# Another sequence for three groups of matmuls: stick-breaking's values, the shared keys and values, banded attention's queries

## The chip, the cores and the metric

The kernel runs on one core of one Trainium2 chip. The metric is the device time of one execution in microseconds (us); the lower the better. TensorE does the matmuls (PE in the profile, its weight loads PEld), VectorE (DVE) and ScalarE (ACT) the elementwise work, GpSimd (POOL) a few small operations and the accumulating loads, and SyncE (SP) issues the plain loads.

## What is computed

A decoder trunk of two layers on 256 rows of 1024 float32 values. Each layer is a half-step SwiGLU FFN, an attention, and another half-step FFN; layer 0 has stick-breaking attention, layer 1 sliding-window attention over keys and values that are computed once, from the stream after layer 0. Cut from the reference:

```python
for layer in range(DEPTH):                     # DEPTH = 2
    h = h + 0.5 * swiglu(rms_norm(h, ffn1_norm[layer]), ffn1_w_in[layer], ffn1_w_out[layer])
    hn = rms_norm(h, mix_norm[layer])
    if layer < N_A_LAYERS:
        qkv = (hn @ sb_w_qkv[layer]).reshape(B, S, 3, SB_HEADS, HEAD_DIM)
        o = stick_breaking_attention(qkv[:, :, 0], qkv[:, :, 1], qkv[:, :, 2])
        h = h + o.reshape(B, S, SB_HEADS * HEAD_DIM) @ sb_w_o[layer]
    else:
        q = rotary((hn @ swa_w_q[j]).reshape(B, S, SWA_Q_HEADS, HEAD_DIM), pos)
        o = sliding_window_sink_attention(q, k_shared, v_shared, swa_sinks[j])
        h = h + o.reshape(B, S, SWA_Q_HEADS * HEAD_DIM) @ swa_w_o[j]
    h = h + 0.5 * swiglu(rms_norm(h, ffn2_norm[layer]), ffn2_w_in[layer], ffn2_w_out[layer])
    if layer == N_A_LAYERS - 1:
        kv = (rms_norm(h, kv_norm) @ kv_w).reshape(B, S, 2, SWA_KV_HEADS, HEAD_DIM)
        k_shared, v_shared = rotary(kv[:, :, 0], pos), kv[:, :, 1]
return rms_norm(h, final_norm)
```

The model has 16 heads of 64, 4 shared key/value heads, a window of 128 and 2816 hidden columns in each FFN.

## The kernel before

**Tiles and precision.** The 256 rows are two tiles (t = 0, 1) of 128. Every dense product runs as three matmuls on split operands: a megabyte of weights lands in a `raw` buffer, ScalarE casts it to `w_hi` in two halves (L335), VectorE subtracts to give `w_lo` (L337), and TensorE adds x_hi w_hi + x_lo w_hi + x_hi w_lo in a PSUM bank (`step`, L354; all matmuls are issued at L224). There are five raw buffers and ten slots of the pool WP for split weights, that is five weights of a hi and a lo.

**Stages.** Four FFNs with the two attentions between them: FFN, stick-breaking, FFN, FFN, banded attention, FFN. At the end of a stage `finish(t)` adds the residual into `hN` (L453), takes the root of the mean square, scales (`xs`, L440), transposes in TensorE (L386) and splits into `xT_h` (L392) and `xT_l` (L393); the next stage's products of tile t need these. An FFN's block 0 is plain (gate and up, tile by tile), block 1 is narrow (256 columns), blocks 2 to 5 are Strassen-like (`strassen`, L607): four weights are loaded, sums of weights are made in the raw buffers, two by VectorE (L618) and two by accumulating loads from GpSimd's queue (`fetch`, L622). `sums` makes their sums of x from the transposes. `out(n)` multiplies a block's result by `w_out`.

**Stick-breaking** (L761). `values(j)` makes one half of the value columns for both tiles; four groups of heads follow, each with a projection of queries and keys (32 steps of three 256-column matmuls) and two `heads` chains of tasks (scores, ScalarE's functions, cumulative sums, values). `values(0)` stands ahead of group 0, `values(1)` ahead of group 2.

**Shared keys and values** (`shared_kv`, L883). `operands` normalizes `hN` with another gain into `xkv_h`, `xkv_l` through the bank `tr`; 48 matmuls in two banks, a rotation (`rotary`, L873) and transposes through `tr` give `kT_s` and `v_s`. It runs inside the third FFN, behind block 0.

**Banded attention** (L917). `queries(c)` makes 256 query columns (four heads) for both tiles in the banks `qb[0]` and `qb[1]`: 24 matmuls for each tile, a rotation on VectorE (L878 to L881), two transposes back into the same bank (L953), a copy to `qT`. `heads(g, i)` handles two heads of group g: scores for both tiles in the banks `zp[n % 2]`, maxima, exponentials, normalization, transposes (L1022 to L1024) and the product with `v_s`. `out_proj` follows an order written out by hand.

**What sets the order.** Nothing is issued as it is written. Each `T(engine, duration, fn, r=, w=, prio=, lat=)` adds a task to `Plan`; dependencies follow from what tasks read and write, in the order in which they are added. `plan.order()` then simulates the engines with these durations and latencies; whenever an engine is free it takes the ready task of the least `prio`, by default `plan.pos`, which advances with the dense work (`dense`). The order found is the order in each engine's queue, and on the chip each queue is strictly in order. Loads have a prio of 30,000 ns (`LOADS`) ahead of their place, splits 7,000 ns (`LEAD`).

## Time and profile before

| | us |
|---|---|
| median of three runs (all: 940.67, 942.66, 942.68) | 942.66 |
| time of the profiled execution | 940.34 |
| its span, first to last instruction | 938.6 |
| TensorE busy in it | 923.9 (98%) |
| VectorE busy | 776.4 (83%) |
| ScalarE busy | 597.3 (64%) |
| GpSimd busy | 51.6 (6%) |

The load queues moved 206.06 MB, 220 GB/s in the mean, and the mean granted clock of TensorE was 0.995. The stages, by the timeline: first FFN to 189 us, stick-breaking to 309, second FFN to 485, third to 677, banded attention to 756, fourth FFN to the end. The ends of matmuls are modelled, so holes in TensorE are read from the starts of its instructions rather than from its busy share. A time beside a wait is idle time of the engine that waits, and the releaser named is the one that came last.

### The profile page before, as it was taken

To read this page: it belongs to the slowest core of one execution; us is meant where nothing else is said; L and a number is where in the kernel's file an instruction comes from. 1 tells how busy PE (TensorE), PEld (TensorE's weight loads), DVE (VectorE), ACT (ScalarE), POOL (GpSimd) and SP (SyncE) were. 2 spreads that over 40 slices of the span, in tenths; PEclk is the share of its full clock that TensorE was granted. 3 is DMA by queue.
4 is the path that set the end of the run, shared out by engine and by line. 5 is a ranking of instruction groups with operands and counts; after the bars stand their busy time and mean duration, and the time that the engine had idled before them with its cause. 6 is when DMAs were issued, how large, how long until landed. Compare 5 with 4: busy or idle time off the path is not lost.

```text
span 938.6 us, 12152 instructions
## 1 busy us (share of the span) xinstructions
PE 923.9 (98%) x4660; PEld 764.2 (81%) x4660; DVE 776.4 (83%) x918; ACT 597.3 (64%) x837; POOL 51.6 (6%) x62
## 2 busy tenths in 40 slices
PE   9999999999999999999999999999999999999997
PEld 7888888788898888888887888888878788888885
DVE  7889998656566887999878789998688598799983
ACT  6567676647567656776566567677756475676662
POOL 1011010000000000110000001010000000011000
PEclk9999999999999999999999999999999999999999
DMA  9988999773434676999965498999642257799961
GB/s 319 365 193 253 270 297 267 244 247 98 171 96 131 204 222 183 248 293 294 313 230 188 137 264 206 304 281 281 231 157 91 90 180 201 202 227 310 274 175 45
DMA packets 100205, 206.06 MB, mean 220 GB/s; under 512 B 3762, under 2 KB 24498, under 8 KB 100147
## 3 DMA queue, kind: packets, MB, share of 16 engines
q1 hardware_dynamic: 83104, 171.46, 52.5%
q0 software_dynamic: 16896, 33.56, 21.0%
q8 instruction: 36, 0.59, 0.2%
q10 hardware_dynamic: 146, 0.27, 0.1%
q14 instruction: 23, 0.18, 0.1%
HBM read 204.22 MB, written 1.05 MB: 219 GB/s over the span
## 4 chain that ended last, share of the span: by engine, by line
PE 57%; DVE 16%; issue 2%; DMA 2%; ACT 1%; POOL 0%; POOLq 0%; DVEq 0%; ACTq 0%
PE ps L224 54%; DVE w_lo L337 10%; DVE raw L618 3%; DMA raw<-in_ffn_w_in_dram 1%; PE ps L522 1%; DMA raw<-in_swa_w_q_dram 1%; PE ps L386 1%; DVE aT_l L393 1%; ACT w_hi L335 1%; DVE u L638 0%; DVE m L641 0%; DVE hN L453 0%; DVE p L638 0%; PE ps L953 0%; DVE xs L440 0%
## 5 line engine op out<-in xcount | busy, mean ns | idle before, releaser
L337 DVE TENSOR_TENSOR w_lo<-raw,w_hi 128x1024 fp32r<-128x1024 f32 x412 | 485.8, 1221 | 57.3 <-ACT w_hi L335 57.1
L335 ACT CAST w_hi<-raw 128x1024 fp32r<-128x1024 f32 x412 | 411.8, 1050 | 123.2 <-PE ps L224 71.5
L224 PE MATMUL ps<-w_hi,xT_h 128*128 128x512 f32 (+1 forms) x480 | 184.3, 384 | 0.1
L224 PE MATMUL ps<-w_hi,xT_l 128*128 128x512 f32 (+1 forms) x480 | 181.0, 377 | 1.0 <-DVE xT_l L393 1.0
L224 PE MATMUL ps<-w_lo,xT_h 128*128 128x512 f32 (+1 forms) x480 | 181.1, 377 | 0.0
L224 PE MATMUL ps<-w_hi,aT_h 128*128 128x512 f32 x352 | 138.8, 394 | 0.0
L224 PE MATMUL ps<-w_lo,aT_h 128*128 128x512 f32 x352 | 137.4, 390 | 0.0
L224 PE MATMUL ps<-w_hi,aT_l 128*128 128x512 f32 x352 | 137.2, 390 | 0.0
L224 PEld LDWEIGHTS ps<-w_hi,xT_l 128*128 128x128 f32 x480 | 91.0, 190 | 16.8 <-DVE xT_l L393 1.4
L224 PEld LDWEIGHTS ps<-w_hi,xT_h 128*128 128x128 f32 x480 | 91.1, 190 | 16.3 <-issue 0.9
L224 PEld LDWEIGHTS ps<-w_lo,xT_h 128*128 128x128 f32 x480 | 90.9, 189 | 16.5
L224 PE MATMUL ps<-w_hi,S_h 128*128 128x512 f32 x256 | 101.6, 397 | 0.0
L224 PE MATMUL ps<-w_lo,S_h 128*128 128x512 f32 x256 | 100.0, 391 | 0.0
L224 PE MATMUL ps<-w_hi,S_l 128*128 128x512 f32 x256 | 99.8, 390 | 0.0
L618 DVE TENSOR_TENSOR raw<-raw 128x1024 f32<-128x1024 f32 x64 | 77.7, 1223 | 1.1
L224 PEld LDWEIGHTS ps<-w_lo,aT_h 128*128 128x128 f32 x352 | 66.1, 188 | 13.9
L224 PEld LDWEIGHTS ps<-w_hi,aT_l 128*128 128x128 f32 x352 | 66.2, 188 | 13.3
L224 PEld LDWEIGHTS ps<-w_hi,aT_h 128*128 128x128 f32 x352 | 66.2, 188 | 13.1
L623 POOL DMA_DIRECT2D raw<-in_ffn_w_in_dram x32 | 41.0, 1282 | 526.8 <-ACT w_hi L335 171.6
L224 PEld LDWEIGHTS ps<-w_lo,S_h 128*128 128x128 f32 x256 | 48.1, 188 | 10.1
L224 PEld LDWEIGHTS ps<-w_hi,S_l 128*128 128x128 f32 x256 | 48.2, 188 | 9.3
L224 PEld LDWEIGHTS ps<-w_hi,S_h 128*128 128x128 f32 x256 | 48.1, 188 | 9.2
(155 smaller groups left out, 1007.8 us busy)
## 6 DMA issues: line engine op xcount, KB each, us to landing
raw<-in_ffn_w_in_dram SPq DMA_DIRECT2D x76, 1024.0 KB, 7.5
raw<-in_ffn_w_out_dram SPq DMA_DIRECT2D x44, 1024.0 KB, 5.0
raw<-in_ffn_w_in_dram POOLq DMA_DIRECT2D x32, 1024.0 KB, 9.2
raw<-in_sb_w_qkv_dram SPq DMA_DIRECT2D x12, 1024.0 KB, 5.3
raw<-in_ffn_w_in_dram SPq DMA_DIRECT2D x16, 512.0 KB, 5.1
raw<-in_ffn_w_in_dram SPq DMA_DIRECT2D x16, 256.0 KB, 5.6
raw<-in_sb_w_o_dram SPq DMA_DIRECT2D x4, 1024.0 KB, 4.9
raw<-in_swa_w_q_dram SPq DMA_DIRECT2D x4, 1024.0 KB, 8.7
```

The lines of the kernel that those rows point to most:

```text
L224: PE.matmul(ps, lhsT=lhsT, rhs=rhs, start=start, stop=stop, skip_group_check=True)
L335: T("ACT", act(m), lambda sl=sl: ACT.copy(out=flat(hi)[:, sl], in_=flat(raw)[:, sl]), r=[(raw, i) for i in rs] + first, w=[(hi, i) for i i ...
L337: T("DVE", dve(m), lambda sl=sl: DVE.tensor_sub(out=flat(lo)[:, sl], in0=flat(raw)[:, sl], in1=flat(hi)[:, sl].bitcast(F32)), r=[(raw, i) ...
L386: PE.transpose(out=bank.ap[:, i * P:(i + 1) * P], in_=s, identity=ident)
L393: T("DVE", dve(n), lambda: DVE.tensor_sub(out=lo[2](), in0=src(), in1=hi[2]().bitcast(F32)), r=B(bank) + [hi[0:2]], w=[lo[0:2]])
L522: PE.transpose(out=tr.ap[:, i * P:(i + 1) * P], in_=m.ap[:, i * P:(i + 1) * P], identity=ident)
L618: T("DVE", dve(m), lambda sl=sl: DVE.tensor_add(out=flat(dst)[:, sl], in0=flat(dst)[:, sl], in1=flat(src)[:, sl]), r=[(src, k) for k in ks ...
L623: T("POOL", 1500, lambda: nc.gpsimd.dma_start(out=dst.ap, in_=src, accum_op=ALU.add), w=[(dst, 0), (dst, 1)], prio=plan.pos - LOADS, lat=F ...
```

## The change

In stick-breaking all four value products come first, both halves for tile 0 and then both for tile 1. In the third FFN the shared keys and values are added behind block 1 and `out(0)` rather than behind block 0, with the position of their operands set back by 8,000 ns. In banded attention queries are made for one group and one tile at a time, in a sequence written out by hand; queries(1, 0) uses a bank of `zp` for its product and `qb[0]` for its transposes. The hand-written order of the output projection takes six of the eight k ahead instead of four. In the planner a plain load is costed at 330 instead of 250 bytes per ns, and an accumulating load no longer at a latency of 10,000 ns but at 500 ns and a stretch of SP's line at 170 bytes per ns, for which no instruction is issued.

```diff
--- before.py
+++ after.py
@@ -36,7 +36,8 @@
 PAIRS = 5
 RAWS = 5
 PIECES = 2
-FETCH = 10000.0
+ADDING = 170.0
+PLAIN = 330.0
 BY_DMA = False
 DMA3 = True
 FSUMS = 5000.0
@@ -295,7 +296,7 @@
 
 
     def dma(src, dst, nbytes, w, prio, name=None):
-        T("SP", nbytes / (300.0 if prio < -8e5 else 250.0), lambda: nc.sync.dma_start(out=dst(), in_=src), w=w, prio=prio)
+        T("SP", nbytes / (300.0 if prio < -8e5 else PLAIN), lambda: nc.sync.dma_start(out=dst(), in_=src), w=w, prio=prio)
 
     def gain(vec):
         g = G4.get([P, D], F32, "gain")
@@ -621,7 +622,8 @@
 
             def fetch(dst, src):
                 T("POOL", 1500, lambda: nc.gpsimd.dma_start(out=dst.ap, in_=src, accum_op=ALU.add), w=[(dst, 0), (dst, 1)],
-                  prio=plan.pos - LOADS, lat=FETCH)
+                  prio=plan.pos - LOADS, lat=500.0)
+                T("SP", P * 2048 * 4 / ADDING, lambda: None, w=[(dst, 0), (dst, 1)], prio=plan.pos - LOADS)
 
             def product(bank, raw, xs, first, last, at=0.0):
                 w = split(raw)
@@ -716,10 +718,10 @@
             if n == 0:
                 if "s" in blocks:
                     sums()
-                if kv:
-                    kv(ring, tr)
             elif n < last and kind != "s":
                 out(n - 1)
+            if kv and n == 1:
+                kv(ring, tr)
         S8.put(SH, SL)
 
 
@@ -772,15 +774,17 @@
             ring.append(ring.pop(0))
             return ring[-1]
 
-        def values(j):
-            ws = [weight([(slice(0, 512), wv[:, 4 * i:4 * i + 4, 2 * D + 512 * j:2 * D + 512 * j + 512])], 4, 512) for i in range(2)]
-            for t in range(NT):
-                b = bank_()
-                for i in range(2):
-                    four(b, ws[i], lambda kk: of_x(t, 4 * i + kk), i == 0, i == 1)
-                    if t == 1:
-                        WP.put(*ws[i])
-                copy_act(lambda t=t: v.ap[:, t, half(j)], lambda b=b: b.ap, 512, B(b), [(v, (t, j))])
+        vw = {}
+
+        def values(j, t):
+            b = bank_()
+            for i in range(2):
+                if (j, i) not in vw:
+                    vw[j, i] = weight([(slice(0, 512), wv[:, 4 * i:4 * i + 4, 2 * D + 512 * j:2 * D + 512 * j + 512])], 4, 512)
+                four(b, vw[j, i], lambda kk: of_x(t, 4 * i + kk), i == 0, i == 1)
+                if t == 1:
+                    WP.put(*vw[j, i])
+            copy_act(lambda: v.ap[:, t, half(j)], lambda: b.ap, 512, B(b), [(v, (t, j))])
 
         def heads(g, i):
             n = 2 * g + i
@@ -835,10 +839,10 @@
                 sl_ = slice(2 * g, 2 * g + 2)
                 part_to(ob, (oh, g, lambda: oh.ap[:, sl_]), (ol, g, lambda: ol.ap[:, sl_]), 512, lambda: two(ob.ap))
 
-        values(0)
+        for t in range(NT):
+            for j in range(2):
+                values(j, t)
         for g in range(4):
-            if g == 2:
-                values(1)
             ws = [weight([(slice(0, 256), wv[:, :, s * D + 256 * g:s * D + 256 * g + 256])], KD, 256) for s in range(2)]
             for b in range(2):
                 ps = bank_()
@@ -888,7 +892,10 @@
                 normed(t, rstds[t], gk, [tr, tr], kh, kl)
 
         def run(ring, tr):
+            at_ = plan.pos
+            plan.pos -= 8000.0
             operands(tr)
+            plan.pos = at_
             wv = by_k(kv_w)
             bs = [ring[0], ring[1]]
             ring[:] = [ring[2], ring[0], ring[1]]
@@ -929,31 +936,39 @@
         NM, SM, ES = [tiny(2 * H) for _ in range(3)]
         T("ACT", 1300, lambda: ACT.preload_act_table_set("natural_log_exp_and_others"), w=[(consts, "tbl")])
 
-        def queries(c):
-            w = weight([(slice(0, 256), wv[:, :, 256 * c:256 * c + 256])], KD, 256)
-            for t in (1, 0) if c else (0, 1):
-                b = qb[t]
-                for k in range(KD):
-                    (sh, sl), keys = of_x(t, k)
-
-                    def run(k=k, sh=sh, sl=sl, b=b):
-                        r_h, r_l = w[0].ap[:, k], w[1].ap[:, k]
-                        mm(b.ap[:, 0:256], sh(), r_h, k == 0, False)
-                        mm(b.ap[:, 0:256], sl(), r_h, False, False)
-                        mm(b.ap[:, 0:256], sh(), r_l, False, k == KD - 1)
-                    dense(360, run, r=[(w[0], k // 4), (w[1], k // 4)] + keys, w=B(b))
-                if t == (0 if c else 1):
-                    WP.put(*w)
-                qr, tmp = STG.get([P, 4, HD], F32, "qr"), STG.get([P, 4, HD], F32, "qr_t")
-                rotary(lambda qr=qr: qr.ap, tmp, lambda b=b: b.ap[:, 0:256].rearrange("p (n d) -> p n d", n=4), t, 2, 4, B(b), B(qr))
-                STG.put(tmp)
-
-                def run(b=b, qr=qr):
-                    for i in range(2):
-                        PE.transpose(out=b.ap[:, i * P:(i + 1) * P], in_=qr.ap[:, 2 * i:2 * i + 2].rearrange("p a d -> p (a d)"), identity=ident)
-                T("PE", 218, run, r=B(qr) + ID, w=B(b))
-                STG.put(qr)
-                copy_act(lambda t=t: qT.ap[:, 2 * c:2 * c + 2, ts(t)], lambda b=b: b.ap[:, 0:256].rearrange("p (a b) -> p a b", a=2), 256, B(b), [(qT, (c, t))])
+        qw = {}
+
+        def queries(c, t):
+            if c in qw:
+                w = qw.pop(c)
+                last = True
+            else:
+                w = qw[c] = weight([(slice(0, 256), wv[:, :, 256 * c:256 * c + 256])], KD, 256)
+                last = False
+
+
+            b, bt = zp[1][0] if (c, t) == (1, 0) else qb[t], qb[t]
+            for k in range(KD):
+                (sh, sl), keys = of_x(t, k)
+
+                def run(k=k, sh=sh, sl=sl):
+                    r_h, r_l = w[0].ap[:, k], w[1].ap[:, k]
+                    mm(b.ap[:, 0:256], sh(), r_h, k == 0, False)
+                    mm(b.ap[:, 0:256], sl(), r_h, False, False)
+                    mm(b.ap[:, 0:256], sh(), r_l, False, k == KD - 1)
+                dense(360, run, r=[(w[0], k // 4), (w[1], k // 4)] + keys, w=B(b))
+            if last:
+                WP.put(*w)
+            qr, tmp = STG.get([P, 4, HD], F32, "qr"), STG.get([P, 4, HD], F32, "qr_t")
+            rotary(lambda: qr.ap, tmp, lambda: b.ap[:, 0:256].rearrange("p (n d) -> p n d", n=4), t, 2, 4, B(b), B(qr))
+            STG.put(tmp)
+
+            def run():
+                for i in range(2):
+                    PE.transpose(out=bt.ap[:, i * P:(i + 1) * P], in_=qr.ap[:, 2 * i:2 * i + 2].rearrange("p a d -> p (a d)"), identity=ident)
+            T("PE", 218, run, r=B(qr) + ID, w=B(bt))
+            STG.put(qr)
+            copy_act(lambda: qT.ap[:, 2 * c:2 * c + 2, ts(t)], lambda: bt.ap[:, 0:256].rearrange("p (a b) -> p a b", a=2), 256, B(bt), [(qT, (c, t))])
 
         def view(buf, t0, t1, h0, h1):
             return buf.ap.rearrange("p (t h) -> p t h", t=2)[:, t0:t1, h0:h1]
@@ -1042,14 +1057,15 @@
                 sl_ = slice(2 * g, 2 * g + 2)
                 part_to(o, (oh, g, lambda: oh.ap[:, sl_]), (ol, g, lambda: ol.ap[:, sl_]), 512, lambda: two(o.ap))
 
-        for g in range(4):
-            queries(g)
-            for i in range(2):
-                heads(g, i)
+
+        for what, a_, b_ in (("q", 0, 0), ("q", 0, 1), ("h", 0, 0), ("q", 2, 0), ("q", 1, 0), ("h", 0, 1),
+                            ("q", 1, 1), ("h", 1, 0), ("h", 1, 1), ("q", 2, 1), ("h", 2, 0), ("h", 2, 1),
+                            ("q", 3, 1), ("q", 3, 0), ("h", 3, 0), ("h", 3, 1)):
+            (queries if what == "q" else heads)(a_, b_)
         T("ACT", 1300, lambda: ACT.preload_act_table_set("silu_and_others"), w=[(consts, "tbl")])
         WP.put(qT)
         out_proj(w_o, oh, ol, [qb, ob], finish,
-                 [(0, range(4), (0, 1)), (1, range(4), (1,)), (0, range(4, 8), (0, 1)), (1, range(4, 8), (1,)), (1, range(8), (0,))],
+                 [(0, range(6), (0, 1)), (1, range(6), (1,)), (0, range(6, 8), (0, 1)), (1, range(6, 8), (1,)), (1, range(8), (0,))],
                  lambda t, k: [(oh, k // 2), (ol, k // 2)])
         S8.put(oh, ol)
 
```

## Rows read from the trace of the kernel before

**Rows 1.** The page, part 1: busy us (share of the span) and instructions.

```profile
PE 923.9 (98%) x4660; PEld 764.2 (81%) x4660; DVE 776.4 (83%) x918; ACT 597.3 (64%) x837; POOL 51.6 (6%) x62
```

**Rows 2.** The chain that ended last: start us, us, what.

```profile
303.31 11.58 PE ps L224 x51
```

**Rows 3.** Timeline, TensorE, 256-column projections: start us, us, engine line op.

```profile
202.15 0.28 PE L224 MATMUL ps<-xT_h,w_hi 128*128 128x256 f32 x1
...
213.55 0.28 PE L224 MATMUL ps<-xT_h,w_lo 128*128 128x256 f32 x1
```

**Rows 4.** TensorE's waits: us in total, times, longest us.

```profile
PE ps L522 <- DVE m L513: 1.7, 1, 1.7
```

**Rows 5.** Timeline, TensorE, entry of stick-breaking, tile 1's values.

```profile
195.37 0.39 PE L224 MATMUL ps<-w_hi,xT_h 128*128 128x512 f32 x1
196.77 0.50 PE L224 MATMUL ps<-w_hi,xT_l 128*128 128x512 f32 x1 [1.01 <-DVE xT_l L393]
```

**Rows 6.** Timeline, TensorE, third FFN, first block.

```profile
507.66 0.39 PE L224 MATMUL ps<-w_lo,xT_h 128*128 128x512 f32 x1
509.78 0.66 PE L522 MATMUL ps<-ident,m 128*128 128x128 f32 x4 [1.73 <-DVE m L513]
```

**Rows 7.** Timeline, TensorE, entry of banded attention.

```profile
679.85 0.28 PE L224 MATMUL ps<-w_lo,xT_h 128*128 128x256 f32 x1
...
681.52 1.32 PE L386 MATMUL ps<-ident,xs 128*128 128x128 f32 x8 [1.40 <-DVE xs L440]
...
683.71 0.56 PE L224 MATMUL ps<-w_hi,xT_h 128*128 128x256 f32 x1
...
686.48 0.28 PE L224 MATMUL ps<-w_hi,xT_h 128*128 128x256 f32 x1
```

**Rows 8.** Windows, entry of banded attention: PE, PEld, DVE, ACT, POOL busy, granted clock, DMA.

```profile
683.70:691.10 7.40, 7.40 (x52) 7.27 (x51) 6.04 (x10) 2.75 (x4) 0.00 (x0) 0.81 0.70 237
```

**Rows 9.** Windows, heads of groups 0 and 1 in stick-breaking.

```profile
213.70:231.90 18.20, 18.20 (x152) 16.63 (x150) 11.23 (x16) 12.10 (x19) 0.00 (x0) 1.00 0.35 116
231.90:249.50 17.60, 17.60 (x102) 13.76 (x102) 10.67 (x15) 12.31 (x19) 0.00 (x0) 1.00 0.36 120
```

**Rows 10.** Timeline, VectorE, third FFN, first block and shared operands.

```profile
500.37 0.75 DVE L440 SCALAR_TENSOR_TENSOR xs<-hN,small,gain 128x512 f32<-128x512 f32 x1
...
503.37 5.76 DVE L337 TENSOR_TENSOR w_lo<-raw,w_hi 128x1024 fp32r<-128x1024 f32 x5
...
516.12 0.69 DVE L393 TENSOR_TENSOR xkv_l<-ps,xkv_h 128x512 fp32r<-128x512 f32 x1 [1.82 <-ACT xkv_h L392]
...
518.63 0.69 DVE L393 TENSOR_TENSOR xkv_l<-ps,xkv_h 128x512 fp32r<-128x512 f32 x1 [1.82 <-ACT xkv_h L392]
```

**Rows 11.** Windows, third FFN up to and through its Strassen blocks.

```profile
512.00:528.00 16.00, 16.00 (x80) 13.26 (x79) 7.77 (x14) 5.51 (x11) 0.00 (x0) 1.00 0.47 161
528.00:546.00 18.00, 18.00 (x87) 14.81 (x86) 17.86 (x24) 11.78 (x17) 1.30 (x1) 1.00 0.71 173
...
546.00:658.00 112.00, 111.90 (x506) 92.43 (x505) 105.14 (x103) 78.52 (x91) 8.92 (x7) 1.00 0.97 274
```

**Rows 12.** Timeline, VectorE, entry of banded attention.

```profile
682.05 0.28 DVE L878 TENSOR_TENSOR qr_t<-ps,rp 128x128 f32<-128x128 f32 x1
...
682.89 0.42 DVE L881 TENSOR_TENSOR qr<-qr,qr_t 128x256 f32<-128x256 f32 x1
...
684.44 2.35 DVE L337 TENSOR_TENSOR w_lo<-raw,w_hi 128x1024 fp32r<-128x1024 f32 x2
```

**Rows 13.** Timeline, VectorE, end of banded attention.

```profile
747.19 1.37 DVE L453 SCALAR_TENSOR_TENSOR hN<-ps,hN 128x512 f32<-128x512 f32 x2 [2.98 <-PE ps L224]
...
754.51 1.28 DVE L393 TENSOR_TENSOR xT_l<-ps,xT_h 128x512 fp32r<-128x512 f32 x2
```

**Rows 14.** The line L623 (accumulating loads), its last row.

```profile
DMA to landing us min/median/max: 8.4/9.2/12.2
```

**Rows 15.** DMA issues: out<-in engine op xcount, KB each, median us to landing.

```profile
raw<-in_ffn_w_in_dram SPq DMA_DIRECT2D x76, 1024.0 KB, 7.5
```

## The prediction

> **What bounds the kernel now.** I read the page first: TensorE counts as busy for 923.9 of 938.6 us [rows 1]. That share says little, since a record lasts longer than the step to the next start: 51 matmuls of 512 columns take 11.58 us, 227 ns each [rows 2], while one record shows 0.39 us; the 256-column ones start every 0.12 us (95 steps from 202.15 to 213.55) [rows 3]. So I looked for starts that come later than this pace. The four FFNs (L459) run on pace nearly throughout; the end is set by the sum of TensorE's work, and only a hole in TensorE can be won. In the list of TensorE's waits no group comes to more than 1.7 us [rows 4]; the timeline gives the holes their true size:
>
> (a) Entering stick-breaking, the second matmul of tile 1's values waits for that tile's `xT_l`: 195.37 to 196.77, 1.40 us instead of 0.23 [rows 5]. Lost: 1.2 us.
>
> (b) In the third FFN's first block the transposes of `m` start 2.12 us after the last matmul instead of 0.23 [rows 6]. Lost: 1.9 us. This wait of the `m` transposes occurs once in the kernel [rows 4], and only this FFN has the shared keys and values behind its first block.
>
> (c) Entering banded attention: 679.85 to 681.52 before the transposes of tile 1's `xs` (1.55 us lost); from there to 683.71 is 2.19 us for eight transposes and a pair (0.8 + 0.1 us on pace), 1.3 us lost; then 12 matmuls take 2.77 us instead of 1.44, 1.3 us lost [rows 7], because the granted clock averages 0.81 there [rows 8], that is half of 2.4 GHz for a part of it. TensorE had just been nearly idle. Together 4.1 us.
>
> **The change, part by part.**
>
> *Values first, by tile.* The same 96 matmuls, 4 loads and 8 casts in another sequence. At the entry there are now 48 matmuls that need tile 0 alone (10.9 us) instead of 24 (5.4 us). Tile 1 was late by 1.2 us, so 5.4 us more cover takes the hole away: **-1.2 us** (from 0 to -1.4, with the slow start behind the transposes). The two more weights needed early take the places in the cast queues that the first query/key weights have now; those are then needed 10.9 us later. What loses its cover: the heads of group 1 were filled by `values(1)`, 48 matmuls of 0.227 us = 10.9 us, and will be filled by group 2's projections, 96 of 0.12 us = 11.5 us. The trace has both kinds of filling: group 0's heads are filled by projections, group 1's by values, and TensorE is busy through both stretches, VectorE at 11.2 of 18.2 and 10.7 of 17.6 us [rows 9]. So 0 there; bounds -0.2 and +0.5.
>
> *Shared keys and values behind the second block.* Nothing is added; the 48 matmuls, the four xs, transposes and copies, two weights and the rotation all move behind 10.9 us of block 1 and 10.9 us of `out(0)`, with the operands queued 8 us ahead. In VectorE's queue the five weight halves from 503.37 on hold back the product `m`, and VectorE is late at that point because it also does the shared xs at 500.37 (0.7 us) after the sums [rows 10]. Without it and with the same mix as FFNs two and four, which show no such wait, the hole closes: **-1.9 us**. What is hidden anew: the operands go through one bank, one after the other, 2.5 us each (xkv_l at 516.12, 518.63) [rows 10], four of them 10 us; they may start when block 1's second transposes have left `tr`, and `out(0)`'s 48 matmuls are 10.9 us long, so they just fit; if not, the ready Strassen products go first. VectorE is half idle in 512 to 528 (7.8 of 16 us), full in 528 to 546, and 94% busy through the Strassen blocks (105.1 of 112 us) [rows 11]. The moved work is about 12 us on VectorE (four xs and four low halves of 0.6, four weight halves of 1.2, two rotations of 1.3); it leaves the half idle stretch for one 14 to 22 us later that is nearly full, and hands its place to work that was done there. I take 0, since both lie ahead of the same Strassen block and TensorE's work between them is unchanged; bounds 0 and +1.9 (a hole like (b) again, behind the rotation and its transposes). If TensorE needs the keys' transposes before VectorE has rotated, everything behind them in its queue waits, the first Strassen products too.
>
> *Banded attention's queries.* At the entry TensorE now has queries(0,0), (2,0) and (1,0) on tile 0: 72 matmuls, 8.6 us, against 24 (2.9 us). Not all can run in the hole. queries(2,0) uses the same bank as (0,0), which comes free after a rotation of 1.26 us (682.05 to 683.31 [rows 12]), two transposes and a copy: 682.6 at the earliest, 684.5 as now. queries(1,0) has a bank of its own, but its weight is third, and the third weight's low halves come from VectorE at 684.4 to 686.7 now [rows 12]; the queue is likely to take one of them into its wait for the root at 680. By my count 72 query matmuls are done at 688.3 instead of 691.1, with the clock not falling, or less: **-2.8 us**, bounds -4.1 (all of (c)) and -0.5 (nothing but part of the clock's loss). A page speaks against this order: the Trainium skill, Perfetto Trace Analysis, Optimizing Tensor Performance (Matmuls), wants independent groups to rotate through different banks so that emptying one overlaps the next group's matmuls. By that rule alone (2,0) would fill nothing and (c) would shrink by (1,0)'s 2.9 us at most; my -2.8 agrees with it.
>
> At the other end the output projection keeps 30 matmuls behind tile 0's last one instead of 36 (the list now takes six k of tile 1 before tile 0's last two): 30 x 0.227 + 0.8 for the transposes = 7.6 us of cover for a chain that takes 8.2 us (hN at 747.19 to the first half of xT_l at 755.15, and 0.2 before it [rows 13]): **+0.6 us**, bounds 0 and +0.9. When exactly the heads run costs nothing as long as the output projection's matmuls remain to fill between them; the stretch of the heads, 691 to 743, has no such hole now, and if that filling ran out each head's latency would show.
>
> *The planner's costs.* PLAIN, ADDING and the shorter latency emit no instruction; they reorder all queues. For an accumulating load the plan has 1.5 + 10 = 11.5 us now, and 1.5 + 0.5 + 6.2 + 2.0 = 10.2 us after when SP's line is free. They land in 8.4 to 12.2, median 9.2 us [rows 14], so both figures are mostly on the safe side. Plain megabytes go from 4.2 + 2.0 to 3.2 + 2.0 us against a median of 7.5 for the FFN's w_in [rows 15], which is hidden by the five raw buffers that are loaded well ahead. I take 0; bounds below.
>
> **Sum** against the profiled execution (span 938.6, time 940.3): -1.2 - 1.9 - 2.8 + 0.6 = -5.3, so 935.0. The median of the runs shown is 942.7, 2.3 us above the profiled one, so the forecast is **937.3 us**. Changes under 0.3% (2.8 us) can't be told from none.
>
> **Rivals.**
>
> 1. *The bank chain wins in banded attention.* (2,0) and (1,0) come too late, and later (1,1), (2,1) and (3,1) queue for one bank: the part gives 0 instead of -2.2 net. For it: VectorE is 82% busy from 683.7 to 691.1 (6.0 of 7.4 us [rows 8]) and every rotation passes through it. Against: (1,0) has its own bank. Time 939.6.
> 2. *The hole (b) moves.* The rotation and transposes of the shared keys meet a full VectorE and TensorE waits 1.9 us before the first Strassen block. For it: 17.9 of 18 us busy in 528 to 546 [rows 11]. Against: the 8 idle us of VectorE in 512 to 528, which other splits can use in its place. Time 939.2. With rival 1 as well: 941.5, no change.
> 3. *Slower: the new load costs are too hopeful.* ScalarE's queue is in order; a cast (L335) placed before its accumulating load lands holds every cast, silu and staging copy behind it, and VectorE, which works behind ScalarE, has about 7 us to spare per FFN [rows 11]. There are 32 such loads. If each is awaited 1.3 us longer (11.5 - 10.2), that is 41.6 us, less 4 x 7 hidden = +14, so 951 us with the gains. It decides from about 8 us lost, 0.25 us per load above the slack. For it: the last load of each FFN lands late (up to 12.2 us), in front of the next stage's weights. Against: the median of 9.2 is below both costs.
>
> **How the numbers follow.** The forecast, all three gains within their bounds (-3.5 to -7.4, 935.3 to 939.2): 0.58. Rival 1: 0.14, rival 2: 0.10, both: 0.06, rival 3: 0.12. Rivals 1 and 2 alone lie just beyond 2.8 us; I count 0.15 of their 0.24 as faster. So faster 0.73, same 0.09 + 0.06 = 0.15, slower 0.12. The range reaches from a little below the best case, for the runs' own spread of 2 us, to where both rivals hold: 933.5 to 942.5.
>
> **What would show it.** (a) no wait of TensorE for xT_l ahead of the first projections, two groups of 24 value matmuls before tile 1's; (b) m's transposes on pace in the third FFN, and no wait near the shared keys' transposes; (c) 256-column matmuls between 680 and 684, the granted clock at 1.00 and the first scores half a us or a us nearer to the last FFN matmul with more query matmuls ahead of them; at the end a wait of about half a us before the fourth FFN. I am wrong if the Strassen stretches grow (112 us each now), or if the heads' stretch takes more time than the entry gives back.

## The result, and the profile after

The changed kernel takes **935.42 us** (median of 6 runs, 934.89 to 937.01) against 941.30 us for the kernel before, run beside it (6 runs): ratio **0.9938, 95% interval 0.9925 to 0.9951**, so 5.9 us faster. The forecast was 937.3 us in a range of 933.5 to 942.5, made of -5.3 us against the kernel before. The profiled execution took 935.5 us with a span of 933.7 us; that is 4.9 us less than the span of before.

Since only a hole in TensorE can be won, the execution is cut into stages at the first matmul of each, read from TensorE's timeline:

```
us                   start  FFN 1   stick-br.  FFN 2   FFN 3   banded  FFN 4 + end
before               11.27  177.77  119.57     176.12  192.37  78.95   182.52
after                12.98  178.00  118.01     176.01  189.99  76.33   182.40
after - before       +1.71   +0.23   -1.56      -0.11   -2.38  -2.62    -0.12
```

The three edited stages give back 6.6 us. The start (up to the first projection) took between 10.6 and 13.7 us in the profiles of this study without regard to the edit, and the first FFN 177.4 to 178.6 us in those profiles of the kernel before with one part that left it alone; the others agree within 0.8 us where nothing is changed, stick-breaking within 0.1, with one exception: banded attention takes 77.79 us in e10_kvw_later, which doesn't edit it, against 78.9 to 79.3 (the reason stands in the last section). So one profile is good for the stages, to about a us, and the runs for the total. Since spans differ by their start, times of two profiles are compared below from the first matmul of the stage. Of all executions, one of e5_old_costs (2,372 us, against 934.7 to 937.5 in its others) lies apart and is in no figure.

Line numbers are those of each kernel: L225 after is L224 before, L968 is L953. Page, part 1, and TensorE's waits (us in total, times, longest), in reply to [rows 1] and [rows 4]:

```profile
PE 923.0 (99%) x4660; PEld 763.0 (82%) x4660; DVE 776.8 (83%) x918; ACT 596.8 (64%) x837; POOL 51.7 (6%) x62
```

```profile
PE ps L523 <- DVE m L514: 1.1, 1, 1.1
...
PE ps L968 <- DVE qr L885: 0.5, 1, 0.5
...
PE ps L387 <- DVE xs L441: 0.2, 1, 0.2
```

The busy share again says nothing. The 1.7 us wait of `m` is replaced by one of 1.1 us, which has the same name but stands elsewhere (below); the wait for `xT_l` ahead of the first projections is gone.

TensorE's timeline at the three entries and at the last one (start us, us; a bracket would show a wait), in reply to [rows 5], [rows 6] and [rows 7]:

```profile
197.56 0.40 PE L225 MATMUL ps<-w_lo,xT_h 128*128 128x512 f32 x1
197.79 1.04 PE L387 MATMUL ps<-ident,xs 128*128 128x128 f32 x8
198.59 0.48 PE L225 MATMUL ps<-w_hi,xT_h 128*128 128x512 f32 x1
...
510.66 0.40 PE L225 MATMUL ps<-w_lo,xT_h 128*128 128x512 f32 x1
510.89 0.60 PE L523 MATMUL ps<-ident,m 128*128 128x128 f32 x4
...
674.99 0.28 PE L225 MATMUL ps<-w_hi,xT_h 128*128 128x256 f32 x1
...
680.62 0.28 PE L225 MATMUL ps<-w_lo,xT_h 128*128 128x256 f32 x1
680.74 1.22 PE L387 MATMUL ps<-ident,xs 128*128 128x128 f32 x8
682.50 0.44 PE L968 MATMUL ps<-ident,qr 128*128 128x128 f32 x2 [0.54 <-DVE qr L885]
682.70 0.36 PE L225 MATMUL ps<-w_hi,xT_h 128*128 128x256 f32 x1
...
689.13 0.70 PE L225 MATMUL ps<-kT_s,qT 64*128 64x256 f32 x4
...
751.09 0.39 PE L225 MATMUL ps<-w_lo,o_h 128*128 128x512 f32 x1
751.32 0.39 PE L225 MATMUL ps<-w_hi,xT_h 128*128 128x512 f32 x1
```

Stick-breaking goes on at pace from its transposes, and the transposes of `m` follow the last matmul after 0.23 us instead of 2.12. Banded attention has 48 query matmuls instead of 24 before tile 1's transposes, which start on pace. Its first scores come 14.14 us after the first query (689.13 - 674.99), as before (14.01) and not nearer, but 96 query matmuls instead of 72 are done by then; the 72nd starts 10.84 us after the first instead of 13.80. The fourth FFN starts on pace, without the wait of half a us that I forecast.

Windows of the same entry and of the Strassen blocks (busy PE, PEld, DVE, ACT, POOL, granted clock, DMA), in reply to [rows 8] and [rows 11]:

```profile
675.00:680.70 5.70, 5.70 (x49) 5.70 (x48) 4.97 (x8) 3.34 (x6) 0.55 (x1) 1.00 0.92 280
680.70:689.10 8.40, 7.82 (x62) 7.08 (x60) 8.12 (x18) 3.92 (x6) 0.00 (x0) 1.00 0.78 256
546.00:652.00 106.00, 106.00 (x482) 87.75 (x481) 102.54 (x101) 75.74 (x90) 8.92 (x7) 1.00 0.94 261
```

TensorE is no longer nearly idle ahead of the transposes, and the clock is granted at 1.00 (2.4 GHz) where it was 0.81 on average. The Strassen blocks are no longer than before: TensorE is busy throughout, and a block of 132 matmuls takes 30.9 us (566.87 to 597.75; before, 568.57 to 599.45, 30.9).

VectorE in the third FFN's first block, in reply to [rows 10], first a line of before that follows the five halves there, then the kernel after:

```profile
509.04 0.68 DVE L513 TENSOR_TENSOR m<-m,ps 128x512 f32<-128x512 f32 x1
```

```profile
505.10 4.62 DVE L338 TENSOR_TENSOR w_lo<-raw,w_hi 128x1024 fp32r<-128x1024 f32 x4
509.64 0.68 DVE L514 TENSOR_TENSOR m<-m,ps 128x512 f32<-128x512 f32 x1
```

This is the row to stop at: weight halves still stand ahead of `m`, and `m` starts 24.64 us after the FFN's first matmul (485.00), *later* than before the change (24.31, from 484.73). The hole is gone all the same, so my reason for it can't be right.

The new wait, in the first FFN's first block; TensorE, ScalarE and VectorE:

```profile
35.99 0.39 PE L225 MATMUL ps<-w_lo,xT_h 128*128 128x512 f32 x1
37.52 0.66 PE L523 MATMUL ps<-ident,m 128*128 128x128 f32 x4 [1.14 <-DVE m L514]
```

```profile
31.16 7.69 ACT L336 CAST w_hi<-raw 128x1024 fp32r<-128x1024 f32 x8 [2.19 <-DMA raw<-in_ffn_w_out_dram]
```

```profile
32.24 4.63 DVE L338 TENSOR_TENSOR w_lo<-raw,w_hi 128x1024 fp32r<-128x1024 f32 x4 [2.55 <-ACT w_hi L336]
36.79 0.68 DVE L514 TENSOR_TENSOR m<-m,ps 128x512 f32<-128x512 f32 x1
```

Eight casts stand in ScalarE's queue; the first waits 2.19 us for a plain load of `w_out`, VectorE's four halves wait behind it, and `m` behind those. TensorE loses 1.3 us (1.53 instead of 0.23).

### The profile page after: what moved, and what is told of

Read it like the earlier page. It is cut to its first block, busy times and chain, and to the rows that moved or that the text cites. A ratio compares the mean times of both kernels' runs of the same rounds, so it can differ in the third digit from the quotient of the medians.

```text
span 933.7 us, 12138 instructions
## 1 busy us (share of the span) xinstructions
PE 923.0 (99%) x4660; PEld 763.0 (82%) x4660; DVE 776.8 (83%) x918; ACT 596.8 (64%) x837; POOL 51.7 (6%) x62
## 4 chain that ended last, share of the span: by engine, by line
PE 87%; DVE 5%; DMA 5%; ACT 1%; issue 1%; SPq 1%; POOL 0%; POOLq 0%; ACTq 0%; DVEq 0%
PE ps L225 84%; DVE w_lo L338 3%; DMA raw<-in_ffn_w_in_dram 3%; PE ps L523 2%; DMA raw<-in_ffn_w_out_dram 1%; PE ps L387 1%; DMA raw<-in_swa_w_q_dram 1%; SPq L299 1%; ACT w_hi L336 1%; DVE e L1030 0%; DVE small L1004 0%; DVE xs L441 0%; DVE hN L454 0%; ACT sq L412 0%; PE ps L1037 0%
## 5 line engine op out<-in xcount | busy, mean ns | idle before, releaser
L225 PE MATMUL ps<-w_hi,xT_h 128*128 128x512 f32 (+1 forms) x480 | 182.9, 381 | 0.0
L225 PE MATMUL ps<-w_lo,xT_h 128*128 128x512 f32 (+1 forms) x480 | 180.2, 375 | 0.0
L225 PE MATMUL ps<-w_hi,xT_l 128*128 128x512 f32 (+1 forms) x480 | 180.1, 375 | 0.0
L225 PE MATMUL ps<-w_hi,aT_h 128*128 128x512 f32 x352 | 139.3, 396 | 0.0
L225 PE MATMUL ps<-w_lo,aT_h 128*128 128x512 f32 x352 | 137.4, 390 | 0.0
L225 PE MATMUL ps<-w_hi,aT_l 128*128 128x512 f32 x352 | 137.0, 389 | 0.0
L225 PEld LDWEIGHTS ps<-w_lo,xT_h 128*128 128x128 f32 x480 | 90.3, 188 | 16.6
L225 PEld LDWEIGHTS ps<-w_hi,xT_l 128*128 128x128 f32 x480 | 90.4, 188 | 15.9 <-DVE xT_l L394 0.2
L225 PEld LDWEIGHTS ps<-w_hi,xT_h 128*128 128x128 f32 x480 | 90.3, 188 | 15.5
L225 PE MATMUL ps<-w_hi,S_h 128*128 128x512 f32 x256 | 101.5, 396 | 0.0
L225 PE MATMUL ps<-w_lo,S_h 128*128 128x512 f32 x256 | 99.9, 390 | 0.0
L225 PE MATMUL ps<-w_hi,S_l 128*128 128x512 f32 x256 | 99.6, 389 | 0.0
L225 PEld LDWEIGHTS ps<-w_lo,aT_h 128*128 128x128 f32 x352 | 66.1, 188 | 14.2
L225 PEld LDWEIGHTS ps<-w_hi,aT_l 128*128 128x128 f32 x352 | 66.2, 188 | 13.2
L225 PEld LDWEIGHTS ps<-w_hi,aT_h 128*128 128x128 f32 x352 | 66.1, 188 | 13.0
L225 PEld LDWEIGHTS ps<-w_lo,S_h 128*128 128x128 f32 x256 | 48.0, 188 | 10.2
L225 PEld LDWEIGHTS ps<-w_hi,S_l 128*128 128x128 f32 x256 | 48.1, 188 | 9.3
L225 PEld LDWEIGHTS ps<-w_hi,S_h 128*128 128x128 f32 x256 | 48.1, 188 | 9.3
```

Of the source, the lines that this page charges most:

```text
L225: PE.matmul(ps, lhsT=lhsT, rhs=rhs, start=start, stop=stop, skip_group_check=True)
```

## Experiments

Ratios are to the kernel before, run beside each; stages are in us.

**One part at a time.** Each of the first four is the kernel before with one part of the change as it stands in the diff; the last two undo the costs.

```diff
e1: values(0) ... if g == 2: values(1)  ->  for t in range(NT): for j in range(2): values(j, t)
e2: kv(ring, tr) behind block 1 (n == 1), operands(tr) planned 8000 ns earlier
e3: queries(c, t) in the written sequence, (1, 0) in zp[1][0]; out_proj's list with range(6)
e4: -FETCH = 10000.0   +ADDING = 170.0   +PLAIN = 330.0   (and the task on SP's line)
```

> The kernel before with the values part alone. Theory of the three holes (each part closes its own hole in TensorE and they add up): the wait for tile 1's xT_l at the entry of stick-breaking goes, 1.2 to 1.6 us less, ratio 0.9983 to 0.9987; stick-breaking takes 118.0 instead of 119.6 us. Theory of the costs (the gain comes from the new order that the planner's costs give everywhere): the hole may close, the total stays, ratio 1.000.

> The kernel before with the shared keys and values behind block 1 alone. Theory of the three holes: the m transposes of the third FFN's first block come on pace, no new wait, 1.9 to 2.4 us less, ratio 0.9975 to 0.9980; the third FFN takes 190.0 instead of 192.4 us. Theory of the costs: ratio 1.000, the hole of 1.9 us stays or comes back behind the rotation of the keys.

> The kernel before with banded attention's sequence and the output projection's list alone. Theory of the three holes: 48 instead of 24 query matmuls ahead of tile 1's transposes, the granted clock at 1.00 throughout the entry, banded attention 76.3 instead of 79.0 us, 2.2 to 2.8 us less, ratio 0.9970 to 0.9977. Theory of the costs: ratio 1.000.

> The kernel before with the planner's new costs alone. Theory of the three holes: all three holes stay and a new one of 1.3 us opens in the first FFN ahead of the m transposes near 37 us, since four more casts are queued there for loads that have not landed: 0 to 1.5 us more, ratio 1.0000 to 1.0016. Theory of the costs: 3 to 6 us less, ratio 0.994 to 0.997.

```
            ratio [95%]              stage that it edits
e1_values   0.9986 [0.9974, 0.9998]  stick-breaking 117.99 (before 119.57)
e2_shared   0.9996 [0.9986, 1.0007]  third FFN 191.15 (192.37)
e3_queries  0.9977 [0.9966, 0.9988]  banded attention 75.67 (78.95)
e4_costs    1.0023 [1.0012, 1.0034]  first FFN 176.84 (177.77), third 192.97, banded 79.76
```

Values do alone what they do in the whole: -1.6 us in the stage. Queries do 0.7 us more alone, -3.3 against -2.6; the whole change with the old costs (e11, below) also has 75.67 us. (In e3 39 query matmuls stand ahead of tile 1's transposes, not the 48 that I expected.) The shared part gives 1.2 instead of 2.4 us, which its runs can't tell from nothing: `m` is on pace, but a Strassen block of the same FFN now waits. TensorE's timeline of e2_shared:

```profile
604.50 0.39 PE L224 MATMUL ps<-w_lo,xT_h 128*128 128x512 f32 x1
605.88 0.66 PE L522 MATMUL ps<-ident,m 128*128 128x128 f32 x4 [0.98 <-DVE m L641]
```

That is 1.15 us lost, in a block where the kernel before loses 0.3: the hole moved, as rival 2 had it, but to another place. The costs alone make the kernel 0.2% slower; of those 2.2 us the stages of the one profile show nothing (their sum is 0.2 us less than before), so where it goes is open. The hole that I expected near 37 us does not open with the costs alone: in the first FFN of e4 no start is more than 0.3 us late.

> The changed kernel with the planner's old costs. Theory of plain addition (the costs alone were 2.2 us worse, so taking them back gains that): 8 us less than before, ratio 0.991. Theory of an interaction (the shared keys' later place pays fully only with the new order, since with the old one a hole of about 1.1 us opens in the third FFN's second Strassen block, as in the run with that part alone): the three parts as measured alone, 1.3 + 0.4 + 2.2 = 3.9 us less, up to 5, ratio 0.9945 to 0.9960; the third FFN takes about 191.2 us instead of 190.0, and the hole of 1.3 us in the first FFN near 37 us is gone.

> The changed kernel with the old planner costs, once more, for its profile. If the new costs bring nothing of their own: ratio 0.994 to 0.995, banded attention 76 to 77 us, stick-breaking 118.0. Theory one: the new costs are what closes the hole at a Strassen block of the third FFN that the shared part alone opened (1.2 us there): then it is there again here and that FFN takes 191.0 instead of 190.0; and they open the hole of 1.3 us in the first FFN's first block: then it is absent here and the first FFN takes 177 instead of 178. Theory two: both holes are chance of each plan and neither follows the costs.

```diff
 e5, e11: the changed kernel with FETCH = 10000.0, 250.0 for plain loads and no task on SP's line
```

Ratios 0.9942 [0.9928, 0.9956] and 0.9941 [0.9925, 0.9957] against 0.9938 for the whole change; the profile is e11's. So beside the three sequences the new costs bring nothing that the runs can tell. e11's profile shows what they do: without them the first FFN's hole at 35.99 is absent, but 0.96 us are lost before the last Strassen block's transposes (171.54), a wait that the changed kernel does not have, and 0.6 us at the third FFN's block of e2 (603.21); the third FFN takes 190.62 us (189.99 with them), banded attention 75.67 (76.33). Holes of about a us are closed and opened, and the sum is nothing. The hole near 37 us needs both the new costs and the new places: it is in the changed kernel, e6 and e7, and not in e4 or e11. The theory of plain addition (0.991 without the costs) falls.

**Banded attention: the bank and the output order.** Both are the changed kernel with one line put back.

```diff
 e6:
-            b, bt = zp[1][0] if (c, t) == (1, 0) else qb[t], qb[t]
+            b, bt = qb[t], qb[t]
 e7:
-  [(0, range(6), (0, 1)), (1, range(6), (1,)), (0, range(6, 8), (0, 1)), (1, range(6, 8), (1,)), ...
+  [(0, range(4), (0, 1)), (1, range(4), (1,)), (0, range(4, 8), (0, 1)), (1, range(4, 8), (1,)), ...
```

> The changed kernel with queries(1,0) in the bank of queries(0,0) and (2,0) again. Theory of the bank chain (the second 24 query matmuls at the entry are queries(1,0), and they run there only because they have a bank of their own): 24 instead of 48 matmuls ahead of tile 1's transposes, a hole of 1.5 us and the half clock are back, 2.0 to 4.0 us more than the changed kernel, ratio to before 0.996 to 0.998. Theory that any tile 0 work fills the hole: as the changed kernel, 0.994.

> The changed kernel with the old hand-written order of the output projection (four k ahead instead of six). Theory of the cover (30 matmuls behind tile 0's last cover less of the chain into the fourth FFN than 36 do): 0.3 to 0.9 us less than the changed kernel, ratio to before 0.993. Theory that the heads end early enough for the order not to matter at the end: within 0.3 us of the changed kernel there, 0.994; if the list sets how the heads are filled, more, banded attention 77 us or longer.

e6: ratio 0.9993 [0.9984, 1.0002], banded attention 80.22 us (76.33). Its timeline of TensorE and windows:

```profile
677.38 0.28 PE L225 MATMUL ps<-w_lo,xT_h 128*128 128x256 f32 x1
680.29 1.96 PE L387 MATMUL ps<-ident,xs 128*128 128x128 f32 x8 [2.63 <-DVE xs L441]
682.14 0.69 PE L968 MATMUL ps<-ident,qr 128*128 128x128 f32 x2
682.48 0.56 PE L225 MATMUL ps<-w_hi,xT_h 128*128 128x256 f32 x1
```

```profile
675.00:681.00 6.00, 3.37 (x27) 3.17 (x26) 5.27 (x9) 3.17 (x6) 0.55 (x1) 0.94 0.82 288
681.00:689.00 8.00, 8.00 (x57) 7.66 (x57) 6.24 (x13) 3.90 (x6) 0.00 (x0) 0.83 0.70 230
```

With one bank only 24 matmuls stand ahead, 2.8 us are lost at the transposes, and behind the idle stretch the clock is again 0.83 on average: within the new sequence the own bank is worth 3.9 us by the stage and 5 us by the runs (0.9993 against 0.9938), nearly the whole change. This is rival 1's mechanism, and dearer than rival 1 had it: without the bank the stage is 1.3 us longer than before, not as long. The rule that I weighed (the Trainium skill, Perfetto Trace Analysis, Optimizing Tensor Performance (Matmuls): independent groups rotate through different banks) holds here, with this number.

e7: ratio 0.9957 [0.9944, 0.9971], banded attention 77.23 us. The old order of the output projection is 0.9 us worse by the stage, so the new one costs nothing. (The intervals of the runs touch, so that it gains isn't shown.) The chain into the fourth FFN is shorter with either list. VectorE before, between tile 0's transposes and its `xT_l` (the row that [rows 13] leaves out), then after:

```profile
752.24 2.35 DVE L337 TENSOR_TENSOR w_lo<-raw,w_hi 128x1024 fp32r<-128x1024 f32 x2
```

```profile
743.11 1.37 DVE L454 SCALAR_TENSOR_TENSOR hN<-ps,hN 128x512 f32<-128x512 f32 x2 [2.98 <-PE ps L225]
...
747.97 1.22 DVE L338 TENSOR_TENSOR w_lo<-raw,w_hi 128x1024 fp32r<-128x1024 f32 x1
749.10 0.69 DVE L394 TENSOR_TENSOR xT_l<-ps,xT_h 128x512 fp32r<-128x512 f32 x1
```

One weight half instead of two stands ahead of `xT_l`, and from `hN` to the end of its first half it is 6.7 us instead of 8.0; e7, with the old list, has the same 6.7 (744.28 to 750.97).

**What made hole (b)?** My reason was VectorE: five weight halves ahead of `m`, and the shared `xs` that made VectorE late. Three edits of the kernel before test it.

```diff
 e8: the shared xs wait for tile 1's m transposes
-  r=[(hN, (t, j))] + B(rstd, g), w=B(xs))
+  r=[(hN, (t, j))] + B(rstd, g) + B(tr), w=B(xs))
 e9: the next block's bank
-            bs = [ring[0], ring[1]]
-            ring[:] = [ring[2], ring[0], ring[1]]
+            bs = [ring[1], ring[2]]
 e10: the shared keys' and values' weights are split behind tile 1's m
-                w = weight([(slice(0, 512), wv[:, 4 * i:4 * i + 4, :])], 4, 512)
+                w = weight([(slice(0, 512), wv[:, 4 * i:4 * i + 4, :])], 4, 512, also=B(m_of[0]))
```

> The kernel before, the shared keys and values still behind block 0, but their scaled rows made to wait for tile 1's m transposes, so that three of them (0.6 to 0.7 us each) leave VectorE's queue ahead of m; the six weight halves ahead of m stay. Theory that the shared rows make VectorE late: the hole of 1.9 us in the third FFN's first block closes to 0.3 us or less, 1.6 to 1.9 us less than before, ratio 0.9980 to 0.9983. Theory that the weight halves alone do it: the hole stays, ratio 1.000.

> The kernel before, with one edit: the shared keys and values take the two banks that follow in the ring instead of the first two, so that the next block's first products get the bank that is free instead of the one that tile 1's product m still reads. VectorE's queue is the same: five weight halves ahead of m. Theory bank (TensorE has nothing to run behind the last matmul because the next block's bank is still read): 45 instead of 36 matmuls stand ahead of m's transposes, 2.0 us more cover, the 1.9 us hole closes, the third FFN takes 190.5 us instead of 192.4, ratio 0.998. Theory weights (five weight halves in VectorE's queue make m late, whatever TensorE has): m comes as late as before; with another place for the transposes the hole opens behind the next nine matmuls, the FFN stays at 192.2 to 192.5, ratio 1.000.

> The kernel before, with one edit: the casts and low halves of the shared keys' and values' two weights wait for tile 1's product m, so two weight halves instead of five stand ahead of m in VectorE's queue; TensorE still has 36 matmuls ahead of m's transposes. Theory weights: m starts 0.2 to 0.4 us after the last matmul's end instead of 1.4, the transposes are on pace, the hole of 1.9 us shrinks to 0.2 at most and the third FFN takes 190.6 us. Theory bank: m is earlier, but its own length and way (0.2 + 0.7 + 0.2 us) stay bare since nothing stands behind the last matmul: a hole of 0.8 to 1.1 us remains; the FFN takes 191.3 to 191.6 us, unless the two weights now come late for the shared products (up to +1). Ratio 0.999 to 1.000 by either.

```
               ratio [95%]              third FFN  matmuls ahead of  the last of    m starts    lost at
                                                   m's transposes    them starts    on VectorE  the transposes
before         1                        192.37      96               22.93          24.31       1.9
e8_xs_later    1.0003 [0.9994, 1.0012]  192.11      96               22.95          24.05       1.6
e9_free_bank   1.0004 [0.9993, 1.0015]  191.81     105               24.97          24.32       0
e10_kvw_later  1.0047 [1.0032, 1.0062]  196.79      96               22.94          23.78       1.4
after          0.9938 [0.9925, 0.9951]  189.99     108               25.66          24.64       0
```

Matmuls and times are counted from the FFN's first matmul (at 484.73, 484.97, 484.90, 485.44 and 485.00 us), up to the transposes of tile 1's `m`; `m` ends and the transposes start 0.7 us after `m` starts, if nothing else holds them. e8 takes the `xs` out of the way, and `m` comes 0.3 us earlier, the hole is 0.3 us smaller: that is the part of the xs in 1.9 us. VectorE and TensorE of e8_xs_later:

```profile
509.02 0.68 DVE L513 TENSOR_TENSOR m<-m,ps 128x512 f32<-128x512 f32 x1
```

```profile
507.92 0.39 PE L224 MATMUL ps<-w_lo,xT_h 128*128 128x512 f32 x1
509.76 0.66 PE L522 MATMUL ps<-ident,m 128*128 128x128 f32 x4 [1.45 <-DVE m L513]
```

e9 leaves VectorE's queue as it was and changes one bank, and the hole closes. VectorE and TensorE of e9_free_bank:

```profile
503.54 5.76 DVE L337 TENSOR_TENSOR w_lo<-raw,w_hi 128x1024 fp32r<-128x1024 f32 x5
509.22 0.68 DVE L513 TENSOR_TENSOR m<-m,ps 128x512 f32<-128x512 f32 x1
```

```profile
509.87 0.39 PE L224 MATMUL ps<-w_lo,xT_h 128*128 128x512 f32 x1
510.10 0.60 PE L522 MATMUL ps<-ident,m 128*128 128x128 f32 x4
...
514.19 0.40 PE L224 MATMUL ps<-w_lo,xT_h 128*128 128x512 f32 x1
515.29 0.66 PE L386 MATMUL ps<-ident,xs 128*128 128x128 f32 x4 [0.70 <-DVE xkv_l L393]
```

The same five halves, the same late `m` (24.32 against 24.31 us), and no hole, since nine matmuls of the next block (2.0 us) stand between. In the kernel before they could not: the shared keys and values take the first two banks of the ring, the next block gets the third, and that is the one that `m` still reads. But e9's gain is gone by the next lines: with the operands going through one bank (`tr`) early, TensorE loses 0.9 us at 514.19 and another 1.1 at 603.79 (0.3 there before), and the third FFN keeps only 0.6 us.

e10 made `m` earlier by only 0.5 us, and the hole smaller by as much, so it isn't the clean test of the weights that it was meant to be. VectorE of e10_kvw_later, and its windows:

```profile
506.94 2.36 DVE L339 TENSOR_TENSOR w_lo<-raw,w_hi 128x1024 fp32r<-128x1024 f32 x2 [3.91 <-ACT w_hi L337]
509.22 0.68 DVE L515 TENSOR_TENSOR m<-m,ps 128x512 f32<-128x512 f32 x1
```

```profile
516.00:521.00 5.00, 1.66 (x10) 1.33 (x9) 2.67 (x4) 0.59 (x1) 0.00 (x0) 0.85 0.99 380
521.00:530.00 9.00, 9.00 (x41) 7.40 (x41) 2.08 (x3) 2.11 (x4) 0.00 (x0) 0.89 0.32 122
```

With three halves fewer VectorE stands idle for 3.9 us, waiting for ScalarE's casts, and so gains little. Even an `m` that starts as the last matmul ends (0.39 us after its start) would, by the same 0.7 us, leave a hole of about 0.9 us (an estimate from these rows): a faster VectorE closes at most half of it, a free bank all. The weights then hold up the shared operands: TensorE is busy for 1.66 of 5 us and the clock falls to 0.85 on average. The third FFN grows by 4.4 us.

**The two costs apart.** The changed kernel with the old figure for plain loads and the new one for accumulating loads.

```diff
-PLAIN = 330.0
+PLAIN = 250.0
```

> The changed kernel with plain loads planned at the old 250 bytes per ns and accumulating loads at the new cost. Theory one: the first FFN's new hole (1.3 us, eight weight casts queued ahead of the silu, one waiting 2.2 us for its load) comes from plain loads planned as faster than they are: it is gone here, the first FFN takes 176.5 to 177.5 us, ratio 0.9925 to 0.9935. Theory two: it comes from the accumulating loads' cost or the new places: it stays, ratio 0.994 to 0.995.

Ratio **1.0347 [1.0327, 1.0367]**: 973.8 us. The hole at 35.99 is gone, as the first theory has it, and the kernel loses 38 us against the changed one, which neither theory had. First FFN 193.5 us, third 203.9. Windows over the same 32 us of the first FFN's Strassen blocks, first e12_plain_250, then the changed kernel:

```profile
92.00:124.00 32.00, 29.95 (x133) 23.67 (x131) 27.73 (x28) 19.08 (x23) 2.55 (x2) 1.00 0.87 249
```

```profile
92.00:124.00 32.00, 32.00 (x147) 26.45 (x145) 31.77 (x33) 22.32 (x28) 2.54 (x2) 1.00 1.00 288
```

TensorE's waits in e12_plain_250, a line that the changed kernel does not have:

```profile
PE ps L225 <- ACT p L636: 11.8, 7, 4.1
```

TensorE, VectorE, ScalarE and the DMA all do less: nothing is the bound, the sequence is worse. Two products that follow each other with only a copy (`p`) between now stand next to each other, and TensorE waits for the copy; these waits are 11.8 of the 38 us, the rest is spread. A count from the code fits it: a Strassen block has six plain loads and two accumulating ones of 1,048,576 bytes; on the planner's SP line that is 6 x 4.19 + 2 x 6.17 = 37.5 us at 250 and 170 bytes per ns, 31.4 us at 330 and 170, and 25.2 us in the kernel before, where accumulating loads took no place on it. A block takes 30.9 us on the chip in the changed kernel (transposes of `m` at 120.34 and 151.23, with 132 matmuls between). By 37.5 the planner holds loads for the bound and would order the engines behind loads that in truth land sooner. That last step is argued from the count, not shown: in e12 ScalarE's casts still wait for loads, 31.5 us in 14 waits against 25.3 in 12 in the changed kernel.

No version ran faster than the changed kernel by more than the runs can tell.

## Why the prediction was right, and where its steps were not

- **Values, -1.2 us:** measured -1.6 in the stage, whole or alone. The wait for `xT_l` is covered by tile 0's second group, and since the stage as a whole is shorter by more than the hole, the heads of group 1 lose nothing that shows. Right, slightly small.
- **Shared keys and values, -1.9 us:** -2.4 in the stage. The size was right and the reason wrong. The step that failed is "VectorE is late at that point because it also does the shared xs ... Without it ... the hole closes": after the change `m` is later (24.64 against 24.31 us after the FFN's first matmul) and the hole is gone. Taking the xs away is worth 0.3 of the 1.9 us (e8), three weight halves 0.5 (e10); nine more matmuls from a free bank close it with `m` as late as before (e9). What was missing was that bank for the next block. I had compared with FFNs two and four, "the same mix", and not looked at what they have there: `m` comes 24.0 and 24.2 us after their first matmul, hardly earlier, but 105 matmuls stand ahead of its transposes instead of 96. That the size came out right is luck: the forecast took the whole hole away, as the change did, by another way. Rival 2 came true in part only without the other parts (e2: 1.15 us at another place); in the whole change that place has no hole.
- **Queries, -2.8 us at the entry:** 24 more matmuls in the same time are 24 x 0.12 = 2.9 us. Right, by the path named: (1,0) has its own bank. I had doubted whether its weight would come in time for the hole ahead of the transposes; it did. The part as a whole, with the output order, gives -2.6 in the stage (-3.3 with the old costs) against -2.2. One premise is weaker than it looks: the 1.3 us of half clock in hole (c) were read from one execution, and with the same hole the clock did not fall in e10 (last section).
- **Output order, +0.6 us:** wrong. The step "7.6 us of cover for a chain that takes 8.2" does not hold after the change: the chain takes 6.7 us from `hN` instead of 8.0, since one weight half and not two stands ahead of `xT_l`, the fourth FFN starts on pace, and the old order gains nothing (e7). It goes with the new sequence of the queries (e3, e6, e7 and e11 have it, e4 not); why the planner orders the weights so was not tried.
- **Planner's costs, 0:** right beside the three sequences, as far as the runs can tell (e5, e11); alone the costs lose 2.2 us (e4), and where is open. Rival 3's mechanism costs TensorE something once, and by a plain load, not an accumulating one: a cast waits 2.19 us for it and TensorE loses 1.3 us. The costs close as much elsewhere (e11). That both costs only work together (e12, +38 us) I had not seen: I compared each with the landing times and did not add up what a block of them takes on the planner's line.

Sum: -1.6 - 2.4 - 2.6 = -6.6 by the stages, -5.9 by the runs, against -5.3. Of the 1.9 us between 937.3 and 935.42, 1.4 come from the kernel before, whose median was 941.30 and not 942.66 beside the changed kernel. One figure of the forecast doesn't follow from its parts: "all three gains within their bounds" ends at -3.5 us, while the bounds given part by part add up to between -7.6 and +0.9.

## What to carry to other kernels

When a matmul or transpose waits for another engine's product, first count what TensorE could run in the meantime and which bank it would need; the product itself may be late in the fast version too. Let the group that fills a gap write to a bank whose reader is long done. A figure in a planner is to be judged with the others that share its line: add up one repeated block and compare it with the block's length in the trace.

## What the runs showed of the hardware

Up to the first projection the same 48 instructions of TensorE took 10.6 to 13.7 us in different executions; two spans can differ by 3 us from this alone.

The granted clock fell to half (1.2 GHz) behind stretches in which TensorE had been partly idle (3.37 of 6 us busy in e6, 1.66 of 5 in e10) and stayed at 1.00 where the gap was filled (7.82 of 8.4 us busy after). But such a stretch does not always bring it. At the entry of banded attention e10_kvw_later has the hole of the kernel before, and its clock stayed at 1.00; its windows there, to be read beside [rows 8]:

```profile
682.00:688.60 6.60, 4.69 (x35) 3.96 (x34) 5.84 (x12) 4.52 (x8) 0.55 (x1) 1.00 0.74 252
688.60:696.00 7.40, 7.36 (x58) 6.55 (x58) 7.13 (x12) 2.75 (x4) 0.00 (x0) 1.00 0.72 244
```

In the kernel before TensorE was busy for 4.67 of the same 6.60 us (677.10 to 683.70), and 0.81 followed. That accounts for e10's 77.79 us instead of 78.95, with nothing changed in the stage: a us of a stage can hang on the clock of one execution. How often the kernel before loses it is not shown. Of the seven profiles with the old entry six have the fall (before, e1, e2, e4, e8, e9). But the granted clock over a whole execution, 0.997 in the profiles of e1, e2, e4 and e9, which have that one fall between start and end, and 0.998 in those that have none (after, e3, e7, e11), is 0.998 or 0.999 in 52 of the 78 executions of the kernel before beside the experiments, which hints that most of them do without it.
